# The seventh product at two levels in the paired part of a Strassen-Winograd matmul with bias and tanh

## The chip, the cores and the metric

The kernel runs on one core of one Trainium2 chip. The metric is the device time of the whole program in microseconds, over all of its work from the inputs in HBM to the stored output.

## The reference

```python
def setup_inputs():
    m, k, n = 4096, 4096, 4096
    return {
        "a": np.random.randn(m, k).astype(np.float32),
        "b": np.random.randn(k, n).astype(np.float32),
        "bias": np.random.randn(n).astype(np.float32),
    }

def reference(a, b, bias):
    return np.tanh(np.matmul(a, b) + bias)
```

## The kernel before

The product is done by Winograd's scheme: seven products, m1 to m7, of quarter-size operands take the place of eight. The output is cut into four column blocks of 1024 columns (`c` = 0 to 3, here "block 0" to "block 3") and sixteen row pairs of 256 rows. An "item" is one row pair in one column block. Its left operands are four quads (`a11`, `a12`, `a21`, `a22`, each 128 x 16 x 128 in fp16) and the sums `s1`, `s2`, `s5`, `s6`, `s7` made from them on DVE (VectorE); its right operands (`b11`, `b22`, `d1`, `d3`, `d4`, `e6`, `e7`) lie in SBUF for the whole column block. A one-level product is sixteen matmuls (`T`) of 128 x 128 by 128 x 512. When an item is met for the first time, the transposed quads are written to a DRAM scratch, with `s2` in place of `a21` and `s5` in place of `a12`; later column blocks fetch them from there.

Some products are split once more, over two items p and q = p + 1 taken together: the rows of p and q, the two halves of the inner dimension, and the two halves of the 512 columns form a 2 x 2 x 2 problem, done by seven products of eight matmuls (`TP`) with 256 columns. The left operands of this second level (`v1` to `v4`, tiles named `h`) are made by DVE for each pair by `left`, each an instruction over 128 x 1024; four places hold them, given out in turn by `place_for`. The right operands (`t1` to `t4`, "forms") are the same for all pairs of a column block. They are either kept in SBUF for the block (`kept_form`, with `t3` written over a quarter of the operand it is made from) or written to DRAM once and streamed back for each use (`put_four` makes them in a staging tile and writes them; `pull_four` fetches the next one on the GpSimd queue as soon as one of the places in `free` is let go by `multiply`).

`TWO` lists the products that are done so in the pairs that `four(n)` handles: m4 and m3 (kept forms in `g` tiles), m2 and m6 (streamed), m5 (kept). m1 and m7 are one-level there (`one_whole`), and m7 adds on to the PSUM bank `z` that holds m1, so one subtraction takes both (`take_m7`). Such pairs make up the later part of blocks 2 and 3: `FOURS`, `begins` and `ends_with` give four pairs in block 2, of which the last hands the operands back for what follows (`leave` is true; m6 and m7 are one-level in it), and six in block 3, of which the last ends the kernel (`last`).

Within `four(n)` the order of all engines' work is written out by hand: `group0` (products 1 and 2), `group1` (products 3 and 4, then two adds that it returns and that are placed later as `w`, `w2` or `u`, `u2`), and `single` for the remaining ones, named 7, 3 and 4. ScalarE copies partial sums between halves of PSUM banks, and puts zeros into a half that is to be accumulated into (`seed`). A bank half "between" holds the second product, shared by three of the four results. `take_d`, `take_c`, `take_m2`, `take_m5`, `take_m1`, `take_m6` and `take_m7` add the results into the output tiles on DVE; `end` and `result` apply tanh on ScalarE and store on the SyncE queue (SP). There are three `o` tiles for results of m2 and m5 of a pair, which need four. `left_over` carries the last steps of a pair into the next (`more`).

`turn_over(c)` is the passage from the ordinary items to these pairs; p and q there are the two items before the first pair, m the pair's first item. It has its own written-out order in which steps of the slot schedule (`at_slot`, 7 slots for an item) are called by `slot(k)`. `STAGED` gives the slots, counted from item p, at which streamed forms are made and written; those at 8 and beyond fall into `turn_over`. `M5_AT` gives the places at which m5's forms are made: negative numbers in `turn_over`, others in the first pair (`forms_at`). `M5_AWAY` is the slot at which the quarter that m5's `t3` overwrites is saved, and `BACK` the steps of the last pair of block 2 at which saved operands return.

`fetch` issues the load of a quad on SP. In `product`, an item in `early_fetch` has the `a12` of the item after next fetched right after the matmuls of m7; `after`, which follows, fetches it for the items in `twos`; p and q of a `turn_over` are in `twos`.

Of the kernel before, what the change touches and what calls it, by code (L numbers as in the profile page):

```python
# [8 lines left out]
P = 128  # L9
QP = 32  # L10
NB = 512
NCW = 2 * NB
# [107 lines left out]
def kernel(  # L120
# [471 lines left out]
    def quarter(what, r, j, i):  # L592

        return bop[TWO[what][1], 2 * r + i][:, :, HALF[j]]

    def four_right(what, name, to, made=None):
        for i in range(2):
            here = to[i] if isinstance(to, list) else to[:, ds(i * TB, TB)]
            of = made[:, ds(i * TB, TB)] if made is not None else None
# [233 lines left out]

    def place_for(what, name):
        k = left_count[0] % 4
        left_count[0] += 1
        owner[k] = what, name
        placed[what, name] = lefts[k]
        return lefts[k]

    def left(n, what, name):
        of = {"v2": "v1", "v4": "v2"}.get(name)
        if of:
            assert (what, of) in owner.values()
            of = by_four(placed[what, of])
        place = by_four(place_for(what, name))
# [12 lines left out]
    def between(n, what):  # L859
        if n not in fours:  # L860
            return bank(n, 0, "w")[:, HALF[TWO[what][3]]]
        i, where, half = {
            "m4": (n, "w", 0), "m3": (n + 1, "w", 0), "m2": (n, "w", 1), "m5": (n + 1, "w", 1),
            "m6": (n, "c", 0),
        }[what]
        return bank(i, 0, where)[:, HALF[half]]

    def multiply(n, what, to, left_, right):
        for t in range(TP):
# [5 lines left out]
            if (what, right) in rights:  # L875
                bt = rights[what, right][:, t]
            else:
# [66 lines left out]

    def m5_form(name):
        if name != "t3":
            pool, tag = (bops, "e6_1") if name == "t1" else (sums, "sum")
            rights["m5", name] = pool.tile([P, TP, NB // 2], fp16, name="form", tag=tag)
        kept_form("m5", name)

    def m5_forms(k):
        for name, at in M5_AT.items():
            if at == k:
                m5_form(name)

# [3 lines left out]
    def give_back(c, step):  # L959
        for (name, part), at in BACK.items():  # L960
            if at == step:
                if name in ("m3", "m4", "m5"):
                    move(name, c, False, part)
# [11 lines left out]
    def four(n):  # L975
# [3 lines left out]
        leave = m not in fours and not last  # L979
        homes.update({"m5": "d", "m6": "w"})  # L980
        pair = {i: items[i][1][0] for i in (p, q)}
        st = {i: state.setdefault((i, 0), {}) for i in (p, q)}
        def forms_at(k):
            if first:
                m5_forms(k)

# [4 lines left out]
        def one_whole(what, i, steps=range(T)):  # L991
            _, left_, right = next(v for v in PRODUCTS.values() if v[0] == what)
            at = "w" if what == "m6" else "z"
            whole(i, left_, right, ((bank(i, 0, at), ds(0, NB)),), what == "m6", steps)

        def end(name, i, r, j):
# [23 lines left out]

        def take_m6(i):
            tt(st[i]["s"], st[i]["s"], bank(i, 0, "w"), ADD)
            end("s", i, 1, 1)

        def take_m7(i):
            tt(st[i]["ds"], st[i]["ds"], bank(i, 0, "z"), SUB)
            end("ds", i, 0, 0)

        step(0)
        group0(n, "m4")  # L1030
        left(n, "m4", "v2")
        more()
        group0(n, "m3")
# [3 lines left out]
        w, w2 = group1(n, "m4")  # L1037
        left(n, "m3", "v3")
        w()
        left(n, "m4", "v4")  # L1040
        u, u2 = group1(n, "m3")
        step(2)
        single(n, "m4", 7)
        w2()
        left(n, "m3", "v4")
        u()
        single(n, "m3", 7)
        u2()
        forms_at(1)
        seed(p, "z", 0)  # L1050
# [12 lines left out]
        left(n, "m5", "v1")  # L1063
        forms_at(2)
        group0(n, "m2")
# [9 lines left out]
        left(n, "m2", "v3")  # L1075
        forms_at(3)
        w, w2 = group1(n, "m2")
        left(n, "m5", "v3")
        w()
        asum(p, "s1")  # L1080
# [5 lines left out]
        single(n, "m2", 7)  # L1086
        forms_at(4)
        w2()
# [20 lines left out]
        step(10)  # L1109
        one_whole("m1", p)  # L1110
        take_m5(q)
        asum(q, "s7")
        if leave:
            take_m1(p)
            if not last:
                fetch(m, "a11")
            for name in ("t1", "t2", "t4"):
                del rights["m5", name]
            step(11)
# [23 lines left out]
        left(n, "m6", "v2")  # L1143
        group0(n, "m6")
        take_m1(p)
# [7 lines left out]
        take_m1(q)  # L1153
        if last:
            for to, half in ((bank(q, 0, "z"), LAST[0]), (bank(p, 0, "c"), LAST[1])):
                tt(to[:, half], bank(q, 0, "z")[:, half], st[q]["ds"][:, half], SUB)
        else:
            fetch(m + 1, "a11")
        one_whole("m7", p)
# [7 lines left out]
        take_m6(p)  # L1167
        if not last:
            fetch(m, "a21")
            fetch(m, "a12")  # L1170
            fetch(m + 1, "a21")
            left(m, "m4", "v1")
            left(m, "m3", "v1")
            take_m6(q)
            seed(p, "w", 0)
            seed(q, "w", 0)
            seed(p, "c", 0)
            one_whole("m7", q)

            def close():  # L1180
                take_m7(q)
                fetch(m + 1, "a12")

            left_over.append(close)
            return
        take_m6(q)
        o = st[q]["ds"]
        for to, half, on in (
            (bank(q, 0, "z"), LAST[0], nc.sync), (bank(p, 0, "c"), LAST[1], nc.scalar)
        ):  # L1190
            whole(q, "s7", "e7", ((to, half),))
            nc.scalar.activation(o[:, half], to[:, half], TANH, scale=-1.0)
            on.dma_start(
                out=out[ds(2 * pair[q] * P, P), ds(c * NCW + half.start, half.size)],
                in_=o[:, half],
            )

# [24 lines left out]
    def turn_over(c):  # L1222
# [28 lines left out]
        product(q, *PRODUCTS[2])  # L1251
        m5_forms(-7)
        single(p, "m4", 3)
# [8 lines left out]
        seed(m, "d", 0)  # L1262
        m5_forms(-6)
        product(q, *PRODUCTS[5])
        fetch(m, "a21")
        slot(12)
        m5_forms(-5)
        slot(13)
        product(p, *PRODUCTS[10])
        m5_forms(-4)  # L1270
        seed(m, "w", 0)
        seed(m + 1, "w", 0)
        fetch(m, "a12")
        left(m, "m4", "v1")
        left(m, "m3", "v1")
        slot(15)
        m5_forms(-3)
        product(q, *PRODUCTS[8])
# [4 lines left out]
        slot(17)  # L1283
        m5_forms(-2)
        seed(m, "c", 0)
        product(q, *PRODUCTS[10])
        fetch(m + 1, "a12")
        free.append("sum")
        pull_four()
        m5_forms(-1)  # L1290

# [470 lines left out]
    for c in FOURS:  # L1762
        if c < NC - 1:
            at_slot(SLOTS * (begins[c] - 2) + M5_AWAY, move, "m5", c, True)

# [55 lines left out]
```

## Time and profile before

| | |
|---|---|
| Median of 3 runs | 1533.37 us (1531.91 to 1534.46) |
| Profiled execution, its own time | 1536.71 us |
| Span of the profile (first to last instruction) | 1535.0 us |
| Mean granted TensorE clock | 0.998 |
| Instructions | 23236 |
| HBM read, written | 331.88 MB, 138.94 MB |
| First pair of block 2 begins | 930.41 us |
| First pair of block 3 begins | 1256.69 us |

The profile is of one execution. Times in it are microseconds from the start of the span unless marked ns. PE is the matmul, PEld the weight load, DVE VectorE, ACT ScalarE, POOL GpSimd, SP SyncE; a "q" behind an engine's name is its instruction queue. A line number is that of the helper that issues the instruction: L475 is the one-level product of ordinary items, L940 (in `whole`) the one-level product in pairs, L879 (in `multiply`) the second-level one, L150 the DVE operation, L309 the fetch of a quad, L821 the fetch of a streamed form, L770 the write of a staged form. In a row of a timeline, "[x <-Y]" is idle time of the engine just before and what ended it. In a row of waits the three numbers are the sum, the count and the longest.

### The profile page before, as it was taken

The page shows a single profiled execution, that of the slowest core. Times are in us where ns is not written, and L with a number is a line of the kernel's source. Part 1 is how long each engine was busy: PE and PEld are TensorE (multiplying, and loading weights), DVE is VectorE, ACT ScalarE, POOL GpSimd, SP SyncE. Part 2 cuts the span into 40 slices and gives each one's busy share as a digit, 9 for nine tenths or more (in the row PEclk, how much of TensorE's full clock was granted, in tenths as well). Part 3 has the DMA queues.
Part 4 walks back from the last instruction along what each step waited for, and adds up shares of the span by engine and source line. Part 5 has one row for each costly group of instructions (what it writes and reads, how often), then busy time and mean ns, then how long its engine had stood idle before and what let it go on. Part 6 is the DMA issues. An engine that isn't in the chain of part 4 may idle for free.

```text
span 1535.0 us, 23236 instructions
## 1 busy us (share of the span) xinstructions
PE 1521.8 (99%) x8805; PEld 862.0 (56%) x8805; DVE 1120.6 (73%) x1531; ACT 361.3 (24%) x762; POOL 477.6 (31%) x868
## 2 busy tenths in 40 slices
PE   9999999999999999999999999999999999999999
PEld 4444444444445666544444556777644556777776
DVE  6789877777876666677787666777658857767777
ACT  3331111111221122111122112232222312323322
POOL 8775443334603231343551121112121211111111
PEclk9999999999999999999999999999999999999999
DMA  9999999999979998999996878899975867888895
GB/s 184 182 204 254 276 245 210 219 209 237 192 219 301 251 285 257 239 259 241 216 184 193 286 246 289 291 328 321 344 255 166 241 231 283 296 306 309 314 340 174
DMA packets 203604, 386.66 MB, mean 252 GB/s; under 512 B 25186, under 2 KB 100194, under 8 KB 203492
## 3 DMA queue, kind: packets, MB, share of 16 engines
q0 software_dynamic: 117232, 198.50, 57.1%
q1 hardware_dynamic: 85588, 186.36, 34.4%
q8 instruction: 69, 1.13, 0.3%
q10 hardware_dynamic: 672, 0.33, 0.1%
q14 instruction: 43, 0.35, 0.1%
HBM read 331.88 MB, written 138.94 MB: 307 GB/s over the span
## 4 chain that ended last, share of the span: by engine, by line
PE 96%; DMA 3%; DVE 1%; issue 0%; ACT 0%; DVEq 0%; ACTq 0%
PE ps L475 58%; PE ps L879 19%; PE ps L940 9%; PE ps L1451 5%; PE ps L672 4%; DMA a<-scratch 2%; DMA out_dram<-o 0%; DVE h L150 0%; DVE a L150 0%; DMA coarse<-in_a_dram 0%; PE warm L1511 0%; DVE form L150 0%; PE tp L1552 0%; DVE ps L150 0%; PE spread L438 0%
## 5 line engine op out<-in xcount | busy, mean ns | idle before, releaser
L475 PEld LDWEIGHTS <-a 128*128 128x128 f16 x3264 | 319.3, 98 | 378.7 <-DMA a<-scratch 0.4
L475 PE MATMUL ps<-b,a 128*128 128x512 f16 x1148 | 262.0, 379 | 0.0
L475 PE MATMUL ps<-e,a 128*128 128x512 f16 x932 | 212.1, 379 | 0.0
L475 PE MATMUL ps<-d,a 128*128 128x512 f16 x896 | 202.5, 379 | 0.0
L879 PEld LDWEIGHTS <-h 128*128 128x128 f16 x1760 | 172.2, 98 | 34.4 <-DVE h L150 10.1
L275 DVE STREAM_TRANSPOSE a<-nat 128x1024 f16<-128x1024 f16 (+2 forms) x202 | 175.3, 911 | 19.1 <-PE ps L475 17.6
L821 POOL DMA_DIRECT2D form<-form_m x133 | 70.4, 529 | 363.8 <-PE ps L879 342.5
L475 PE MATMUL ps<-d,s 128*128 128x512 f16 x656 | 148.3, 379 | 0.0
L879 PEld LDWEIGHTS <-a 128*128 128x128 f16 x1320 | 129.8, 98 | 24.7 <-issue 0.8
L475 PEld LDWEIGHTS <-s 128*128 128x128 f16 x848 | 83.0, 98 | 97.7
L247 POOL DMA_DIRECT2D nat<-in_a_dram x176 | 92.9, 533 | 134.0 <-DVE a L275 64.0
L378 POOL DMA_DIRECT2D b<-in_b_dram x192 | 103.4, 544 | 83.8 <-DVE a L275 31.0
L150 DVE TENSOR_TENSOR ps<-ps,x 128x256 f32<-128x256 f32 x128 | 54.2, 431 | 89.7 <-PE ps L879 42.3
L150 DVE TENSOR_TENSOR a<-a,a 128x2048 f16<-128x2048 f16 (+1 forms) x97 | 115.8, 1203 | 0.2
L940 PEld LDWEIGHTS <-a 128*128 128x128 f16 x688 | 66.7, 98 | 70.9 <-issue 0.3
L879 PE MATMUL ps<-form,h 128*128 128x256 f16 x768 | 98.2, 276 | 6.0 <-DVE h L150 5.8
L499 ACT ACTIVATE o<-ps 128x512 f32<-128x512 f32 x90 | 54.1, 601 | 160.9 <-issue 104.4
L940 PE MATMUL ps<-e,a 128*128 128x512 f16 (+2 forms) x360 | 77.7, 370 | 0.0
L150 DVE TENSOR_TENSOR h<-a,h 128x1024 f16<-128x1024 f16 x110 | 75.2, 685 | 0.0
L475 PE MATMUL ps<-side,a 128*128 128x512 f16 x288 | 73.9, 379 | 0.0
L940 PE MATMUL ps<-d,a 128*128 128x512 f16 x320 | 72.2, 379 | 0.0
L879 PE MATMUL ps<-form,a 128*128 128x256 f16 x536 | 70.3, 275 | 0.0
(179 smaller groups left out, 1838.5 us busy)
## 6 DMA issues: line engine op xcount, KB each, us to landing
a<-scratch SPq DMA_DIRECT2D x144, 512.0 KB, 7.0
form<-form_m POOLq DMA_DIRECT2D x133, 512.0 KB, 6.0
out_dram<-o SPq DMA_DIRECT2D x203, 256.0 KB, 5.7
nat<-in_a_dram POOLq DMA_DIRECT2D x288, 128.0 KB, 6.4
scratch<-a SPq DMA_DIRECT2D x48, 512.0 KB, 6.3
b<-in_b_dram POOLq DMA_DIRECT2D x160, 128.0 KB, 5.5
scratch<-a SPq DMA_DIRECT2D x32, 256.0 KB, 5.8
cast<-in_b_dram POOLq DMA_DIRECT2D x64, 128.0 KB, 9.1
```

The source lines that it names most:

```text
L150: nc.vector.tensor_tensor(out=out_, in0=in0, in1=in1, op=op)
L247: nc.gpsimd.dma_start(out=tl[ds(q * QP, QP), :, :], in_=src.rearrange("(mb p) k -> p mb k", p=QP),)
L275: nc.vector.transpose(dst[:, ds(b0 * tb, n * tb), :].rearrange("P (b t) (mb p) -> P mb b t p", t=tb, p=QP), src[:, :, ds(b0, n), :].rearra ...
L378: nc.gpsimd.dma_start(out=dst[ds(q * QP, QP), ds(t, nt)], in_=src)
L475: nc.tensor.matmul(st[where], at, bt, start=(what == "m2" or n < LEAD and what == "m1") and i == 0, stop=i == len(ts_) - 1, skip_group_che ...
L499: nc.scalar.activation(o, src, TANH)
L672: nc.tensor.matmul(to, at, bt, start=False, stop=t == TP - 1, skip_group_check=True)
L821: nc.gpsimd.dma_start(out=rights[what, name], in_=forms[what, name])
L879: nc.tensor.matmul(to, at, bt, start=False, stop=t == TP - 1, skip_group_check=True)
L940: nc.tensor.matmul(to[:, half], at[:, t // TB, t % TB], bop[right, t // TB][:, t % TB, half], start=anew and t == 0, stop=t == T - 1, skip ...
L1451: nc.tensor.matmul(mb[m % 4, j], aq[m, kt // T][:, kt % T, :], right(kt, j), start=fresh and kt == k0, stop=stop and kt == k1 - 1, skip_gr ...
```

## The change

m7 joins the products at two levels in the pairs of `four`. Its forms `t1` and `t2` lie in the tile `side` (the places of `b11` and `e6`, block 0), `t4` in the single `sum` tile of the pool `spare`, which was the sixth place of the streamed forms, and `t3` over a quarter of `e7`, which is saved and brought back in block 2. m7's result goes to the `d` banks, its second product to half of q's `c` bank; m1 is now taken from `z` by itself (`take_m1`, `less_m1`), and m7 by `take_m7` from `d`. Behind m1(p) the steps of m6 and m7 alternate. The places of the left operands are given out differently: `v3` takes the place of `v1`, `v4` that of `v2`. m5's forms are made earlier, four in `turn_over`; those of m7 one there and three in the first pair. The last staged forms are made at slots 4 and 7 instead of 5 and 10 (block 2) and 10 and 13 (block 3). In the pairs, the quads of the next pair are fetched earlier, `a12` of m right after the second-level matmuls that read the old one; in `turn_over` the two fetches of `a12` are taken out and m and m + 1 are put into `early_fetch`. The very end of the kernel, where the last m7 was cut into 384 and 128 columns, now ends with product 4 of m7.

```diff
-       "m2": ("s2", "b11", "z", None), "m5": ("s5", "b22", "d", None)}
+       "m2": ("s2", "b11", "z", None), "m5": ("s5", "b22", "d", None), "m7": ("s7", "e7", "d", None)}
...
-STAGED = {2: (-13, -7, -5, 0, 2, 5, 10), 3: (-8, -6, -4, 1, 10, 13)}
+STAGED = {2: (-13, -7, -5, 0, 2, 4, 7), 3: (-8, -6, -4, 1, 4, 7)}
...
-M5_AWAY = -14
+AWAY = {"m5": -14, "m7": -3}
...
-M5_AT = {"t1": -2, "t3": 1, "t2": 2, "t4": 3}
+KEPT_AT = {
+    ("m5", "t1"): -7, ("m5", "t3"): -6, ("m5", "t2"): -3, ("m5", "t4"): -1,
+    ("m7", "t1"): -4, ("m7", "t2"): 0, ("m7", "t4"): 1, ("m7", "t3"): 2,
+}
...
-    ("m4", "t3"): 5, ("m3", "t3"): 12,
+    ("m4", "t3"): 5, ("m3", "t3"): 12, ("m7", "t3"): 1,
...
-    def place_for(what, name):
-        k = left_count[0] % 4
-        left_count[0] += 1
+    def place_for(n, what, name):
+        first = {"v3": "v1", "v4": "v2"}.get(name)
+        if first and n in fours:
+            k = next(i for i in range(4) if owner.get(i) == (what, first))
+        else:
+            k = left_count[0] % 4
+            left_count[0] += 1
...
-            "m6": (n, "c", 0),
+            "m6": (n, "c", 0), "m7": (n + 1, "c", 0),
...
+    def resident(what, name):
+        if what == "m7" and name in ("t1", "t2"):
+            j = ("t1", "t2").index(name)
+            rights[what, name] = [side[:, :, ds(j * NB + i * NB // 2, NB // 2)] for i in range(2)]
+        elif name != "t3":
+            pool, tag = (bops, "e6_1") if (what, name) == ("m5", "t4") else (
+                (sums if what == "m5" else spare), "sum"
+            )
+            rights[what, name] = pool.tile([P, TP, NB // 2], fp16, name="form", tag=tag)
+        kept_form(what, name)
...
+        def take_m7(i, anew=False):
+            tt(st[i]["ds"], st[i]["ds"], bank(i, 0, "z" if leave else "d"), SUB)
+            if anew:
+                seed(i, "d", 0)
+            end("ds", i, 0, 0)
+
+        def less_m1(i):
             tt(st[i]["ds"], st[i]["ds"], bank(i, 0, "z"), SUB)
-            end("ds", i, 0, 0)
...
         single(n, "m2", 3, 4)
         step(9)
         take_m2(p)
-        asum(p, "s7")
+        asum(q, "s1")
         single(n, "m5", 3)
-        asum(q, "s1")
         if not last:
             fetch(m + 1, "a22")
         take_m2(q)
+        take_m5(p)
+        seed(p, "d", 0)
+        seed(q, "c", 0)
         asum(q, "s6")
         if not leave:
             left(n, "m6", "v1")
-        take_m5(p)
+        asum(p, "s7")
         single(n, "m5", 4)
         step(10)
         one_whole("m1", p)
         take_m5(q)
...
         left(n, "m6", "v2")
         group0(n, "m6")
+        asum(q, "s7")
+        left(n, "m7", "v1")
         take_m1(p)
         if not last:
             fetch(m, "a11")
+        left(n, "m7", "v2")
+        one_whole("m1", q)
         left(n, "m6", "v3")
-        one_whole("m1", q)
+        less_m1(p)
+        group0(n, "m7")
+        left(n, "m7", "v3")
         w, w2 = group1(n, "m6")
+        take_m1(q)
+        if not last:
+            fetch(m + 1, "a11")
+            fetch(m, "a21")
         left(n, "m6", "v4")
         w()
...
+        u, u2 = group1(n, "m7")
         if not last:
-            seed(p, "d", 0)
+            fetch(m, "a12")
+        less_m1(q)
+        left(n, "m7", "v4")
         single(n, "m6", 7)
         w2()
+        u()
+        if last:
+            single(n, "m7", 7)
+            u2()
+            here = bank(q, 0, "d")[:, HALF[0]]
+            tt(here, here, st[q]["ds"][:, HALF[0]], SUB)
...
+            single(n, "m6", 3)
+            take_m6(p)
+            single(n, "m6", 4)
+            take_m6(q)
+            single(n, "m7", 3)
+            take_m7(p)
+            single(n, "m7", 4)
+            nc.scalar.activation(o[:, HALF[0]], here, TANH, scale=-1.0)
+            store_half(o, q, 0, nc.sync)
+            return
+        single(n, "m7", 7)
+        u2()
         single(n, "m6", 3)
-        take_m7(p)
+        single(n, "m7", 3, 4)
+        fetch(m + 1, "a12")
+        seed(p, "c", 0)
+        take_m7(p, True)
+        left(m, "m4", "v1")
         single(n, "m6", 4)
...
+        fetch(m + 1, "a21")
+        take_m6(p, True)
+        take_m7(q)
+        left(m, "m3", "v1")
+
+        def close():
+            take_m6(q, True)
+
+        left_over.append(close)
...
+        early_fetch.update((m, m + 1))
...
-        fetch(m, "a12")
...
-        fetch(m + 1, "a12")
-        free.append("sum")
-        pull_four()
-        m5_forms(-1)
+        resident_at(-1)
```

More of the change, by code (lines that the diff above doesn't have):

```diff
@@ L845, in left @@
             of = by_four(placed[what, of])
-        place = by_four(place_for(what, name))
+        place = by_four(place_for(n, what, name))
         if name == "v1":
@@ L943, in whole, with resident_at @@
                 )
[L945 to L952, printed above, removed]
+    def resident(what, name):
[8 more added lines that the diff above has]
+        kept_form(what, name)
+    def resident_at(k):
+        for form, at in KEPT_AT.items():
             if at == k:
-                m5_form(name)
+                resident(*form)
     def seed(n, where, half):
@@ L994, in one_whole, with store_half @@
             whole(i, left_, right, ((bank(i, 0, at), ds(0, NB)),), what == "m6", steps)
+        def store_half(o, i, j, queue):
+            queue.dma_start(
+                out=out[ds(2 * pair[i] * P, P), ds(c * NCW + HALF[j].start, HALF[j].size)],
+                in_=o[:, HALF[j]],
+            )
         def end(name, i, r, j):
@@ L1186, in four @@
[L1186 to L1196, printed above, removed]
+        u()
[4 more added lines that the diff above has]
+            tt(here, here, st[q]["ds"][:, HALF[0]], SUB)
+            o = st[q]["ds"]
+            tt(o[:, HALF[1]], o[:, HALF[1]], bank(q, 0, "d")[:, HALF[1]], SUB)
+            nc.scalar.activation(o[:, HALF[1]], o[:, HALF[1]], TANH)
+            store_half(o, q, 1, nc.sync)
+            single(n, "m6", 3)
[8 more added lines that the diff above has]
+            return
@@ L1266, in turn_over @@
         slot(12)
-        m5_forms(-5)
+        resident_at(-5)
         slot(13)
         product(p, *PRODUCTS[10])
-        m5_forms(-4)
+        resident_at(-4)
         seed(m, "w", 0)
         seed(m + 1, "w", 0)
-        fetch(m, "a12")
         left(m, "m4", "v1")
@@ L1763 @@
         if c < NC - 1:
-            at_slot(SLOTS * (begins[c] - 2) + M5_AWAY, move, "m5", c, True)
+            for what, at in AWAY.items():
+                at_slot(SLOTS * (begins[c] - 2) + at, move, what, c, True)
     handed = {s for c in FOURS for s in range(SLOTS * (begins[c] - 2) + 8, SLOTS * ends_with[c])}
```

63 lines of the change are left out of this document (21 added, 42 removed).

## The prediction

> **What bounds the kernel.** I read the page first, then the chain of work in order of time, then a table by stage over the two-level pairs, then the timelines of each engine inside one of them.
>
> ```profile
> span 1535.0 us, 23236 instructions
> PE 1521.8 (99%) x8805; PEld 862.0 (56%) x8805; DVE 1120.6 (73%) x1531; ACT 361.3 (24%) x762; POOL 477.6 (31%) x868
> PE 96%; DMA 3%; DVE 1%; issue 0%; ACT 0%; DVEq 0%; ACTq 0%
> ```
>
> TensorE is on the chain 96% of the time, so work taken from it counts in full as long as nothing else becomes late. The next table cuts two-level pairs into stages: the first column is the stretch, then its length, then busy time of PE, PEld, DVE, ACT and POOL, the granted clock, and DMA.
>
> ```profile
> 1398.96:1443.34 44.38, 44.38 (x347) 33.66 (x345) 32.90 (x52) 13.10 (x33) 7.41 (x14) 1.00 0.86 308
> 1256.70:1310.20 53.50, 48.28 (x347) 35.02 (x346) 41.19 (x66) 14.85 (x38) 9.51 (x18) 0.94 0.79 277
> ...
> 1398.80:1412.77 13.97, 13.97 (x129) 12.53 (x128) 9.01 (x16) 4.26 (x12) 0.94 (x2) 1.00 0.73 283
> 1412.77:1423.25 10.48, 10.48 (x98) 9.39 (x96) 8.75 (x15) 2.97 (x8) 2.77 (x6) 1.00 0.84 287
> 1423.25:1443.18 19.93, 19.93 (x123) 11.75 (x120) 15.14 (x23) 5.87 (x14) 3.70 (x7) 1.00 0.96 338
> 944.39:958.75 14.36, 11.32 (x99) 9.05 (x96) 12.44 (x21) 2.54 (x8) 2.75 (x6) 1.00 0.73 252
> 1273.35:1290.09 16.74, 13.55 (x99) 10.79 (x96) 13.03 (x21) 2.94 (x8) 2.76 (x6) 0.80 0.59 188
> ```
>
> An ordinary pair takes 44.38 us and PE is busy for all of it. Its last three rows of stages are m4 and m3 (13.97), m2 and m5 (10.48), and m1, m6, m7 (19.93). The first pair of column block 3 takes 53.50, 9.1 more; the m2/m5 stage alone takes 16.74 there. In block 2 the same stage takes 14.36, 3.9 more than 10.48.
>
> **The change: matmuls.** Pieces of the chain (start, length, what):
>
> ```profile
> 1398.96 24.45 PE ps L879 x224
> ...
> 1433.82 3.45 PE ps L940 x16
> ```
>
> A 256-column matmul takes 24.45/224 = 0.109 us, a product of sixteen 512-column ones 3.45. m7 of a pair is two such products, 6.90 us; at two levels it is 7 x 8 matmuls of 256 columns, 6.11 us. Block 2 has three such pairs (the fourth hands back and keeps the one-level m7), block 3 has six: **9 x 0.79 = 7.1 us less**.
>
> The Trainium skill, "TensorE: Matmul & The Clock Gate", section "Back-to-back issue gap", speaks against this: it gives sustained spacings of 81 ns for 128 columns and 131 ns for 512, so about 98 ns for 256 as an estimate, by which 56 x 98 ns would be more than 32 x 131 ns. The two rows above measure both shapes here, 109 and 216 ns, and the measurement decides.
>
> **DVE in the new tail.** Starts, durations and waits on DVE in an ordinary pair (m1 of p starts on PE at 1423.25; I count t from there):
>
> ```profile
> 1421.95 0.68 DVE L150 TENSOR_TENSOR ds<-ds,ps 128x512 f32<-128x512 f32 x1
> 1422.54 2.36 DVE L150 TENSOR_TENSOR a<-a,a 128x2048 f16<-128x2048 f16 x2
> 1424.81 0.69 DVE L150 TENSOR_TENSOR ds<-ds,ps 128x512 f32<-128x512 f32 x1
> ...
> 1428.98 0.69 DVE L150 TENSOR_TENSOR o<-s,ps 128x512 f32<-128x512 f32 x1 [0.43 <-DMA out_dram<-o]
> 1429.59 0.68 DVE L150 TENSOR_TENSOR ds<-ds,ps 128x512 f32<-128x512 f32 x1
> ...
> 1431.32 0.69 DVE L150 TENSOR_TENSOR h<-a,h 128x1024 f16<-128x1024 f16 x1
> 1431.92 0.68 DVE L150 TENSOR_TENSOR s<-s,ps 128x512 f32<-128x512 f32 x1
> ...
> 1438.18 0.43 DVE L150 TENSOR_TENSOR ps<-ps,x 128x256 f32<-128x256 f32 x1 [2.63 <-PE ps L879]
> 1438.52 0.68 DVE L150 TENSOR_TENSOR ds<-ds,ps 128x512 f32<-128x512 f32 x1
> ```
>
> From start to start a staged left or a 512-column take costs 0.60, a whole sum (s1, s6, s7) 1.13, a small add 0.34. The change adds per pair four lefts (2.4), two adds (0.7) and two takes of m1 apart from m7 (1.2): 4.3 us on 32.9 of 44.4, giving 37.2 of 43.6. DVE is not the bound on average; order decides.
>
> The new PE order in t: m1(p) 0 to 3.45, m6's first two 5.20, m1(q) 8.65, m7's first two 10.40 (the second, on v1, from 9.52), m6's next two 12.14, m7's 13.89, the two sevens 15.63, m6's three 16.51, m7's three and four 18.25, m6's four 19.13. The next pair starts at 19.13 in place of 19.93.
>
> DVE up to m7's v1: take_m2(p) at -1.30 as now, s1(q) -0.70, take_m2(q) 0.43, take_m5(p) 1.03, s6(q) 2.23, m6 v1 3.36 to 4.05 (PE needs it at 4.33), s7(p) to 5.09. take_m5(q) can start at 5.09, but its output buffer is the one that take_m2(p) is storing from: in the quoted pair the store had landed at W = 1428.98 - 1423.25 = 5.73. Then 1.2 for take_m5(q), 0.6 for m6 v2, 1.13 for s7(q), 0.7 for m7 v1: ready at W + 3.6, with PE wanting it at about 9.4. Today W = 5.3 + the wait that the view shows, and a wait up to 0.5 is free in the new order; more is PE idle. The waits in the ordinary pairs of block 2, of block 3, and in the pair that hands back:
>
> ```profile
> DVE o L150 <- DMA out_dram<-o: 1.7, 2, 1.4
> ...
> DVE o L150 <- DMA out_dram<-o: 2.0, 3, 0.8
> ...
> 1099.74 0.69 DVE L150 TENSOR_TENSOR o<-s,ps 128x512 f32<-128x512 f32 x1 [2.88 <-DMA out_dram<-o]
> ```
>
> (us, times, longest.) Block 2: 1.4 and 0.3, so 0.9 lost; block 3: 0.8, 0.8 and 0.4, so 0.6: **1.5 us given back**. If no store were late it is 0; if all were as late as the last row, 2.4 in each pair.
>
> After m7 v1 every left is early: m7 v2 is done at 10.5 (needed 13.0), v3 at 12.3 (14.8), v4 at 15.0 (16.5); the shared third x is free after w2 at 15.4, so u ends at 16.3, needed at 16.5. take_m7(p) follows m7's three by about 0.2, as the add at 1438.18 follows its seven: 17.6 to 18.3, the seed of d on ACT to 18.7, before the next pair's 19.13. take_m6(p) ends at 19.5 and its seed at 19.9, needed at 20.0; take_m6(q) at 21.3, its seed 21.7, needed at 21.75. These margins are 0.1; I charge 0.1 a pair, **0.8**, with 0 and 0.4 a pair as ends. The 1.9 us by which DVE enters the next pair later fall into its idle time there.
>
> **Queues.** On SP the fetches of a21 and a12 of m now wait for m6 v4 and m7 v4 (t 13.5 and 15.0) with only the fetches and stores of the tail behind them; before, they left at 17.7 or later, so they land earlier. POOL streams the forms of m2 and m6 through five places instead of six. The tightest are then the sixth and seventh of m2, asked for 8.5 us before their use; at that point of the pair they land in:
>
> ```profile
> DMA to landing us min/median/max: 3.5/4.2/4.9
> ...
> DMA to landing us min/median/max: 3.4/5.6/8.9
> ```
>
> That costs nothing; the longest of the second row, which is over the ordinary pairs of block 3, would cost under 1 us each.
>
> **The first pairs.** Lines of DVE, SP and PE around the change-over into block 3, then of block 2:
>
> ```profile
> 1256.76 1.29 DVE L150 TENSOR_TENSOR stage<-e,stage 128x1024 f16<-128x1024 f16 x2 [9.53 <-DMA form_m<-stage]
> ...
> 1276.83 0.69 DVE L150 TENSOR_TENSOR h<-a 128x1024 f16<-128x1024 f16 x1 [4.09 <-DMA a<-scratch]
> ...
> SPq L309 <- DMA a<-scratch: 9.1, 1, 9.1
> ...
> 1261.40 10.58 DMA a<-scratch
> 1272.00 4.81 DMA a<-scratch
> ...
> PE ps L879 <- DVE h L150: 3.2, 1, 3.2
> PE ps L879 <- ACT ps L957: 1.9, 1, 1.9
> ...
> SPq L309 <- DMA a<-scratch: 14.1, 2, 8.0
> ...
> 933.08 9.00 DMA a<-scratch
> 942.09 4.19 DMA a<-scratch
> ...
> PE ps L879 <- DVE h L150: 2.7, 2, 1.6
> ```
>
> In block 3 DVE stands 9.53 us before a staged form whose predecessor is still being written out. Everything behind it is late: the take of m7, the seeds (1.9 us of PE), the stores ahead of the last fetches on SP. The new STAGED slots (4 and 7 in place of 10 and 13) take this wait away. The second stall comes from a12 of m+1. It is fetched twice into one tile, by `after` and again by `turn_over`, so the second waits for the first (9.1 us on SP), lands 4.81 later, and only then can DVE form m5's v1. The change drops the call in `turn_over`, but sets `early_fetch`, so `product` and `after` now both fetch: **still two**. With SP free earlier I get: a12(m) behind m7(p), which ends two products (6.9) before the pair begins at 1256.7, so at 1250; its double 8 later at 1258, two stores, a21 and a12 of m+1 at 1259.6, landed 9.0 to 10.6 later, the double another 4.2 to 4.8: 1272.8 to 1275.0. PE wants m5's v1 at 1256.7 + 13.97 + 0.87 = 1271.5 and gets it 0.75 after the landing: 2.0 to 4.2 idle, where it is 3.2 plus 1.9 now. The m7 t3 form (1.3 us) delays m2's v4 by 0.8, and small margins take 0.5. So about 4.2 of the 9.1 stay: **4.9 less**. The forms of m5 move ahead of the pair, where DVE waits for PE anyway, and four of m7 come in; five of these eight now lie before the pair, and the two lefts they delay wait for fetches anyway. Block 2 has no long staged wait and the same double fetch (8.0 on SP, then 4.19), so its loss stays: **0.2 less**, between 2 more and 2 less.
>
> The clock was 0.80 over the 16.74 us: 3.3 us lost beside the 3.2 idle. A wait of 1.6 us in block 2 left it at 1.00. The Trainium skill, same page, Part 1 ("The HAM clock gate"), has the clock halve after an idle window of 3.4 us that runs freely; the trace agrees (3.2 tripped it, 1.6 did not), and by it my 2.0 to 4.2 may go either way.
>
> **The end.** After the last matmul there now stand m7's take of p, two tanh and two stores, where today there is one tanh of 128 columns:
>
> ```profile
> 1531.29 0.49 ACT L1192 ACTIVATE ds<-ps 128x384 f32<-128x384 f32 x1 [1.25 <-PE ps L940]
> 1532.18 0.28 ACT L1192 ACTIVATE ds<-ps 128x128 f32<-128x128 f32 x1 [0.40 <-PE ps L940]
> ```
>
> p's take ends as the last matmul does, its tanh takes 0.6, the other 0.35, so the last store leaves 0.6 later than now after the last matmul: **0.6 given back** (0 to 1).
>
> **Sum.** -7.1 + 1.5 + 0.8 + 0.6 - 4.9 - 0.2 = -9.3. Against the profiled execution (1536.7, with 1.7 around its span) that is 1527.4; against the median of the runs, 1533.4, it is 1524.1. The median lies 3.3 below the profiled run, as much as the half clock cost, so ordinary runs may not have it; then 1527.3. I take 1525.0; its own range is 1521 to 1529.
>
> **Rivals.** (a) The first pairs come clean: with SP early enough both doubles are hidden. Then 9.1 and 4.2 go, but for 1: -16.5, 1517. For it: the stalls are set by a single landing. Against: both fetches stay. (b) The half clock trips in both first pairs: block 3 gains 1.7, block 2 loses 3.1: 1530.6. For it: block 2 idles a little longer, block 3 is near 3.2. (c) Slower: the store of take_m2(p) sets m7 v1 in every pair. If DVE's wait is 2.9 each time, as in the pair that hands back, 9 x 2.4 = 21.6 is lost instead of 1.5: 1544. It outweighs everything from a mean wait of 1.7. For it: the DMA share is 0.96 in this stage. Against: five waits of seven, none over 1.4. (d) The change gains nothing in the first pairs and head margins cost 0.4: 1531 to 1534. (e) 256-column matmuls cost too much per instruction, as the quoted section would have it: break-even is 6.90/56 = 0.123 us, and with its spacings the time is about 1543; the chain's 0.109 leaves it no chance.
>
> **Chances.** Forecast 0.54, (a) 0.10, (b) 0.14, (c) 0.10, (d) 0.12, (e) 0. The range 1517.5 to 1532.5 takes in the forecast, (b), half of (a) and most of (d). Beyond 0.2% (3.1 us, about what a measurement of this kernel can tell from no change): faster 0.79, within 0.10 (part of (d) and (b)), slower 0.11.
>
> **What would show it.** Ordinary pairs of 43.6 us, with PE waiting on DVE h by fractions; no DVE wait on a staged form in the change-over; the second a12 fetch still waiting on SP for the first, and PE idle 2 to 4 us at m5's v1 in both first pairs. Pairs over 44.4 would prove me wrong by (c); first pairs under 46, by (a).

## The result and the profile after

The median fell from 1533.02 us (four runs, 1531.91 to 1534.46) to **1521.9 us** (four runs, 1520.41 to 1523.23): ratio 0.9927, 95% interval 0.9909 to 0.9944, so 11 us or 0.73% faster. The profiled execution took 1522.57 us, its span 1520.6. Of all executions reported below, one, of the change with the old slots, took 2678.31 us at a granted clock of 0.556, and its kernel's ratio leaves it out.

The head of the page after: the span, the busy times, and the chain that ended last.

```profile
span 1520.6 us, 23784 instructions
PE 1509.8 (99%) x9005; PEld 878.9 (58%) x9005; DVE 1166.8 (77%) x1619; ACT 377.1 (25%) x809; POOL 479.1 (32%) x868
PE 91%; DMA 4%; DVE 3%; POOL 1%; issue 0%; ACT 0%; DVEq 0%; SPq 0%; ACTq 0%; POOLq 0%
```

DVE has 46 us more to do and TensorE 12 us less, in more and shorter matmuls. TensorE is still the bound, but its share of the chain fell from 96% to 91%: what is left of waiting sits mostly in transfers (4%) and DVE (3%).

The table by stage after, with the columns of the prediction's. Its rows are, in order: an ordinary pair of block 3, the first pair of block 3, the m2/m5 stage of block 2's first pair, the m4/m3 stage and the m2/m5 stage of block 3's first pair, and a pair of block 3 with a wait.

```profile
1296.18:1339.77 43.59, 43.59 (x371) 35.97 (x368) 36.94 (x61) 14.73 (x39) 7.43 (x14) 1.00 0.90 324
1250.29:1296.18 45.89, 44.38 (x369) 35.70 (x368) 40.11 (x66) 12.86 (x34) 6.89 (x13) 1.00 0.84 278
...
942.85:954.29 11.44, 10.85 (x98) 9.22 (x96) 11.23 (x19) 2.61 (x8) 2.77 (x6) 1.00 0.79 269
1250.29:1264.46 14.17, 14.13 (x129) 12.53 (x128) 11.22 (x20) 4.26 (x12) 0.94 (x2) 1.00 0.68 227
1264.46:1276.85 12.39, 10.94 (x98) 9.23 (x96) 11.23 (x19) 2.61 (x8) 2.78 (x6) 1.00 0.85 270
...
1339.77:1383.87 44.10, 43.77 (x371) 35.94 (x369) 36.84 (x61) 14.74 (x39) 7.43 (x14) 1.00 0.87 307
```

An ordinary pair went from 44.38 to 43.59, the 0.79 of two products in smaller pieces. The first pair of block 3 went from 53.50 to 45.89, its m2/m5 stage from 16.74 to 12.39, and the clock in it is 1.00 where it was 0.80. The same stage of block 2 went from 14.36 to 11.44. In the pair of 44.10, m7's v1 (the first left operand of the second-level m7) comes late. Four of TensorE's five waits on DVE in block 3 after, from its timeline:

```profile
1266.37 1.05 PE L889 MATMUL ps<-form,h 128*128 128x256 f16 x8 [0.87 <-DVE h L153]
1273.24 1.05 PE L889 MATMUL ps<-form,h 128*128 128x256 f16 x8 [0.59 <-DVE h L153]
1374.25 1.05 PE L889 MATMUL ps<-side,h 128*128 128x256 f16 x8 [0.33 <-DVE h L153]
1461.98 1.05 PE L889 MATMUL ps<-side,h 128*128 128x256 f16 x8 [0.36 <-DVE h L153]
```

The first two rows are m5's v1 and m2's v4 in the first pair; the other two (`side` holds m7's first forms) are m7's v1, and a fifth like them, of 0.36, is in the last pair. Ahead of the late v1 of 1374.25, DVE stands at the take of m5, whose output tile is still being stored:

```profile
1370.44 0.69 DVE L153 TENSOR_TENSOR o<-s,ps 128x512 f32<-128x512 f32 x1 [0.91 <-DMA out_dram<-o]
```

In the five pairs behind the first these waits of DVE are 0.34, 0.91, 0.42, 0.94 and 0.94. The two short ones cost TensorE nothing, the three long ones 0.33 to 0.36. In DVE's list of waits (us, times, longest) the staging tile has shrunk to

```profile
DVE stage L153 <- DMA form_m<-stage: 0.8, 1, 0.8
```

where one wait in the passage was 9.53. SP's queue around the change-over after (start, length, what), and then the chain there:

```profile
1250.64 0.86 SPq L493 DMA_DIRECT2D out_dram<-o  x2
1251.60 9.76 SPq L312 DMA_DIRECT2D a<-scratch  x3
```

```profile
1252.19 8.83 DMA a<-scratch
1261.04 4.56 DMA a<-scratch
```

The three fetches take 9.76 us to issue because the last of them waits for the transfer before it: a12 of m + 1 is still fetched twice into one tile, 8.83 us and then 4.56.

**The budget of the profiled span, 14.4 us less.** From matmul to matmul the first pair of block 3 went from 53.35 to 45.89 and that of block 2 from 48.40 to 44.98: beside the 0.79 of the matmuls that is 6.7 and 2.6 less. The nine pairs give 7.1 less. Three waits at m7's v1 cost 0.5 each, the pair that hands back 0.5 (TensorE waits 0.41 for a left there, not followed further), the end 1.9. And block 2's pairs begin at 928.67 in place of 930.41, a lead of 1.7 that is there by 90 us, where the change touches nothing, so it is a difference between executions. -6.7 - 2.6 - 7.1 + 1.5 + 0.5 + 1.9 - 1.7 = -14.2. Without the start it is -12.5, beside -11.1 in the medians; the profiled run of before was 3.7 above its median.

### The profile page after: what moved, and what is told of

It reads as the page before. It is cut to its first block, busy times and chain, and to the rows that moved or that the text cites. A ratio compares the mean times of both kernels' runs of the same rounds, so it can differ in the third digit from the quotient of the medians.

```text
span 1520.6 us, 23784 instructions
## 1 busy us (share of the span) xinstructions
PE 1509.8 (99%) x9005; PEld 878.9 (58%) x9005; DVE 1166.8 (77%) x1619; ACT 377.1 (25%) x809; POOL 479.1 (32%) x868
## 4 chain that ended last, share of the span: by engine, by line
PE 91%; DMA 4%; DVE 3%; POOL 1%; issue 0%; ACT 0%; DVEq 0%; SPq 0%; ACTq 0%; POOLq 0%
PE ps L478 58%; PE ps L889 21%; PE ps L1488 4%; PE ps L950 4%; PE ps L678 4%; DMA a<-scratch 2%; DMA out_dram<-o 1%; DVE h L153 1%; DVE a L153 1%; DVE ps L153 0%; DMA land<-in_a_dram 0%; DVE ds L153 0%; DMA side<-in_b_dram 0%; POOL land L1529 0%; POOL side L1577 0%
## 5 line engine op out<-in xcount | busy, mean ns | idle before, releaser
L478 PEld LDWEIGHTS <-a 128*128 128x128 f16 x3264 | 319.2, 98 | 379.0 <-DMA a<-scratch 0.5
L889 PEld LDWEIGHTS <-h 128*128 128x128 f16 x2048 | 199.2, 98 | 31.8 <-DVE h L153 6.3
L889 PEld LDWEIGHTS <-a 128*128 128x128 f16 x1536 | 150.3, 98 | 24.0
L153 DVE TENSOR_TENSOR ps<-ps,x 128x256 f32<-128x256 f32 x146 | 60.8, 429 | 60.2 <-ACT x L895 32.8
L153 DVE TENSOR_TENSOR h<-a,h 128x1024 f16<-128x1024 f16 x128 | 86.7, 684 | 0.0
L889 PE MATMUL ps<-form,a 128*128 128x256 f16 x608 | 77.5, 273 | 0.0
L153 DVE TENSOR_TENSOR ds<-ds,ps 128x512 f32<-128x512 f32 (+1 forms) x94 | 63.6, 678 | 17.3 <-PE ps L889 7.0
L153 DVE TENSOR_TENSOR h<-a 128x1024 f16<-128x1024 f16 x80 | 54.7, 688 | 16.4 <-DMA a<-scratch 15.7
```

Of the source, the lines that this page charges most:

```text
L153: nc.vector.tensor_tensor(out=out_, in0=in0, in1=in1, op=op)
L478: nc.tensor.matmul(st[where], at, bt, start=(what == "m2" or n < LEAD and what == "m1") and i == 0, stop=i == len(ts_) - 1, skip_group_che ...
L889: nc.tensor.matmul(to, at, bt, start=False, stop=t == TP - 1, skip_group_check=True)
```

## Experiments

The ordinary pairs need no more explanation. The first pairs do: 9.3 us came from two of them, where 5.1 was forecast. Theory A: the new slots of the staged forms did it, by taking DVE's 9.53 us at a staged form (the "staged wait" below) out of the passage. Theory B: the earlier making of m5's forms did it. Theory C: the landing times scatter, and most of it is luck. What remains in these pairs should be the doubled fetch. Excess of the first pair over an ordinary pair of the same kernel (44.38 or 43.59), in block 2 and in block 3, was 4.0 and 9.0 before, 1.4 and 2.3 after. Each excess is read from one profiled run, and the one of before lies 3.7 us above its median and holds the half clock. So the medians say what an edit is worth, and the excess says where.

**The change with the old slots.**

```diff
-STAGED = {2: (-13, -7, -5, 0, 2, 4, 7), 3: (-8, -6, -4, 1, 4, 7)}
+STAGED = {2: (-13, -7, -5, 0, 2, 5, 10), 3: (-8, -6, -4, 1, 10, 13)}
```

> The changed kernel with the staged forms at their former slots (the last ones at 5 and 10 in block 2, at 10 and 13 in block 3). Theory A, the staged slots give what the first pairs gained beyond the matmuls (6.8 us in block 3, 2.8 in block 2): DVE again stands about 9 us before a staged form in the passage into block 3, the first pair there is back at 50 to 53 us (45.9 in the changed kernel), that of block 2 at 46 to 48 (45.0), and the time is 5 to 9 us above the changed kernel, about 1528. Theory B, the earlier forms of m5 give it: under 1.5 us of difference. Theory C, it is all in the second-level m7 and in scatter: no difference.

1530.55 us beside 1533.77 of before, ratio 0.9975 (0.9966 to 0.9984). Without the new slots the change keeps 3 to 4 of its 11 us, so they carry 7 to 8. DVE around the change-over, from its timeline:

```profile
1253.40 1.29 DVE L153 TENSOR_TENSOR stage<-e,stage 128x1024 f16<-128x1024 f16 x2 [6.72 <-DMA form_m<-stage]
1273.27 0.69 DVE L153 TENSOR_TENSOR h<-a 128x1024 f16<-128x1024 f16 x1 [3.42 <-DMA a<-scratch]
```

Both old stalls are back, at 6.72 and 3.42 us where the kernel before had 9.53 and 4.09. Excess 3.3 and 6.2.

**The kernel before with the new slots alone** (the same edit the other way).

> The kernel before with the staged forms at the new slots and nothing else. Theory A: the DVE wait of 9.5 us goes, the first pair of block 3 falls from 53.5 to about 47, that of block 2 by about 2, and the time falls by 5 to 9 us, to about 1526. Theory B (the earlier forms of m5): the first pairs stay within 1.5 us of what they were, 1532 to 1533.

1527.93, ratio 0.9957 (0.9944 to 0.9970). The staged wait is 0.7, and the left that had waited 4.09 us for the doubled fetch waits 1.13:

```profile
1269.78 0.69 DVE L150 TENSOR_TENSOR h<-a 128x1024 f16<-128x1024 f16 x1 [1.13 <-DMA a<-scratch]
```

Excess 2.5 and 2.0: one line of slot numbers gives 5.8 us, most of it in block 3.

**The kernel before with m5's forms made early.**

```diff
-M5_AT = {"t1": -2, "t3": 1, "t2": 2, "t4": 3}
+M5_AT = {"t1": -7, "t3": -6, "t2": -3, "t4": -1}
...
-            pool, tag = (bops, "e6_1") if name == "t1" else (sums, "sum")
+            pool, tag = (bops, "e6_1") if name == "t4" else (sums, "sum")
```

> The kernel before with the forms of m5 made in the passage as in the changed kernel (t1, t3, t2, t4 in this order, t4 in the place that t1 had), nothing else. Theory A: no more than 1 us either way, since the passage into block 3 still waits for the staged form; the added DVE work may even make the seeds later. Theory B: the first pairs lose most of their excess, 1525 to 1528.

1532.48, ratio 0.9993 (0.9984 to 1.0003): no measurable gain, although the excess is 1.1 and 5.5 in the profiled run (1528.89, its fastest of twelve up to 1536.86). The staged wait is still there (longest 7.8), and now it holds the very first products. TensorE in the timeline, and then two stretches in the table of windows:

```profile
1252.37 1.04 PE L879 MATMUL ps<-d,a 128*128 128x256 f16 x8
1255.64 1.03 PE L879 MATMUL ps<-g,h 128*128 128x256 f16 x8 [2.23 <-ACT ps L957]
1256.74 1.80 PE L879 MATMUL ps<-d,a 128*128 128x256 f16 x8
1258.34 1.91 PE L879 MATMUL ps<-g,h 128*128 128x256 f16 x8
```

```profile
1252.00:1258.00 6.00, 3.70 (x26) 2.61 (x25) 5.24 (x9) 2.31 (x6) 1.70 (x4) 0.90 0.49 145
1258.00:1262.00 4.00, 4.00 (x28) 3.10 (x27) 3.27 (x6) 0.94 (x3) 0.42 (x1) 0.72 1.00 366
```

TensorE waits 2.23 us for a seed, and then eight matmuls that take 1.04 take 1.80 and 1.91. So in this run the early forms shorten block 2's first pair, where the excess fell from 4.0 to 1.1, and leave most of block 3's. The median shows no gain, and since this run was 3.6 us faster than it, the excess of an ordinary run may be larger; no run here shows where.

**Both edits in the kernel before**, m7 still at one level.

> The kernel before with both the new slots of the staged forms and the earlier forms of m5; m7 stays one-level. If the first pairs' gain is these two together, the first pair of block 2 takes about 45.5 us and that of block 3 about 46.3, the ordinary pairs stay at 44.38, and the time is near 1525; the changed kernel is then below it by what m7 brings net: 7.1 less for the matmuls, 1.6 back for stores that land late, 1.9 back at the end, about 3.5 us. If the second-level m7 with its order shortens the first pairs by itself, this kernel stays near the 1528 of the new slots alone.

1523.92, ratio 0.9942 (0.9928 to 0.9955): 8.8 of the 11 us without the change's title. Excess 0.0 and 2.6. Block 2 shows what each edit does. TensorE's waits on a left in the m2/m5 stage of its first pair, first in the kernel before (two rows: m5's v1 and m2's v4), then with the new slots alone, then with the early forms alone:

```profile
947.06 1.05 PE L879 MATMUL ps<-form,h 128*128 128x256 f16 x8 [1.63 <-DVE h L150]
955.14 1.05 PE L879 MATMUL ps<-form,h 128*128 128x256 f16 x8 [1.02 <-DVE h L150]
```

```profile
953.76 1.05 PE L879 MATMUL ps<-form,h 128*128 128x256 f16 x8 [1.02 <-DVE h L150]
```

```profile
944.52 1.05 PE L879 MATMUL ps<-form,h 128*128 128x256 f16 x8 [0.93 <-DVE h L150]
```

The early forms take away the wait at m2's v4, which stood behind a form made in the stage. The new slots take away the wait at m5's v1: DVE starts this left 14.4 us into the pair instead of 15.9, and 14.4 instead of 16.4 in the change with the new slots and the old. With both edits TensorE waits for neither. By which path the slots bring the fetch forward in block 2 is not shown.

C, scatter alone, falls: the gains stand in the medians, outside their intervals. But landing times do scatter. In block 3, DVE starts m5's v1 between 13.7 and 16.3 us into the first pair in five profiles with the new slots and the doubled fetch, and between 19.2 and 20.1 in three with the old slots. So the sizes of single waits in one profile are partly luck. What m7 itself gives, with the new order around it, is the difference to the whole change, 2.0 us in the medians, where about 3.5 was expected (3.6 between the two profiled runs from the first pair on), and 1.9 between the early forms alone and the change with the old slots.

**The change with one fetch of each a12.**

```diff
-        early_fetch.update((m, m + 1))
```

> The changed kernel with a12 of the first pair fetched once instead of twice in each passage (m and m + 1 are not put into the list that makes the product fetch it too). By the prediction the second fetch, which waits for the first and lands 4.6 us after it, sets the start of m5's v1: without it DVE has no wait there, PE no idle time before m5's second product in block 3 (0.9 us shown, 1.0 with the rest), and the first pair of block 3 takes about 44.5 us instead of 45.9, that of block 2 about 44.5 instead of 45.0: 1.0 to 2.5 us less, about 1520. If instead DVE's backlog behind the new forms sets it (the 0.6 us waits before m2's v4 in both blocks), the first pairs stay within 0.5.

1520.28, ratio 0.9914 (0.9901 to 0.9926). Excess 0.5 and 0.2; the first pair of block 3 and its m4/m3 and m2/m5 stages:

```profile
1249.89:1264.02 14.13, 14.09 (x129) 12.49 (x128) 12.59 (x23) 4.26 (x12) 0.90 (x2) 1.00 0.45 181
1264.02:1274.50 10.48, 10.48 (x98) 9.39 (x97) 10.09 (x17) 2.93 (x8) 2.81 (x6) 1.00 0.82 278
1249.89:1293.68 43.79, 43.75 (x370) 36.01 (x369) 40.18 (x66) 12.93 (x34) 6.88 (x13) 1.00 0.77 279
```

The m2/m5 stage is at its 10.48 again, so in this profile the doubled fetch was almost all that was left in block 3. Two kernels below keep the doubled fetch and show 1.2 and 0.8 there instead of 2.3, so its price varies from run to run; in the medians it is 1.6 us.

**The kernel before with one fetch of each a12.**

```diff
-        fetch(m, "a12")
         left(m, "m4", "v1")
...
-        fetch(m + 1, "a12")
         free.append("sum")
```

> The kernel before with a12 of m and of m + 1 fetched once in the passage. If the doubled fetch is a cause by itself, the a12 of m + 1 lands 4.8 us earlier in block 3 and 4.2 in block 2, the stall of 3.2 us and the half clock behind it (3.3) go and 1.9 stay: 6.5 less in block 3, 2.5 less in block 2, 1524 to 1525. If the staged form's wait of 9.5 us is what matters, because it makes SP late anyway, a wait of 1 to 3 us stays before m5's first form: 3 to 5 less in all, 1528 to 1530. If both had only one cause, nothing changes: 1533.

1525.8 beside 1533.13, ratio 0.9954 (0.9941 to 0.9967). The doubled fetch was a cause by itself, though the staged wait stayed almost whole. DVE, then what TensorE loses to it:

```profile
1251.35 1.29 DVE L150 TENSOR_TENSOR stage<-e,stage 128x1024 f16<-128x1024 f16 x2 [8.61 <-DMA form_m<-stage]
...
1254.23 1.03 PE L879 MATMUL ps<-g,h 128*128 128x256 f16 x8 [0.99 <-ACT ps L957]
1275.24 1.05 PE L879 MATMUL ps<-form,h 128*128 128x256 f16 x8 [0.37 <-DVE h L150]
```

Excess 0.8 and 2.3. So DVE's wait of 8.6 us costs TensorE little when the fetches behind it are not doubled, and the doubling costs less when DVE does not wait (at m5's v1 TensorE lost nothing with the new slots alone, 2.07 with both edits): each of the two edits alone, slots or fetch, takes 7.0 or 6.7 us off block 3's excess of 9.0, because most of the stall needed both. In the medians, block 2 included, the slots give 5.8 us and the single fetch 7.3.

**The change with a later take of m5.** `take_m5(q)` stands behind m7's v1, as its output tile is the one that is late.

```diff
         single(n, "m5", 4)
         step(10)
         one_whole("m1", p)
-        take_m5(q)
         if leave:
+            take_m5(q)
...
         left(n, "m7", "v1")
+        take_m5(q)
         take_m1(p)
```

> The changed kernel with the take of m5 for q moved behind m7's v1 on DVE (in pairs where m7 is two-level). The prediction holds that the store of m2's result for p, whose buffer this take needs, sets the start of m7's v1: three ordinary or last pairs of block 3 show PE idle 0.33 to 0.36 there and take 44.1 us instead of 43.58. With the move v1 is ready at about 7.5 us after m1 of p begins, 2 before its use, these idle times go and all ordinary pairs take 43.58: 1.0 to 1.6 us less than the changed kernel, if nothing else becomes late. If DVE's amount of work and not the store sets it, the waits come back at another left and the time stays.

1520.19, ratio 0.9917 (0.9903 to 0.9930). No wait at m7's v1 is left; of TensorE's waits on a left only those in the first pairs remain:

```profile
PE ps L889 <- DVE h L153: 1.1, 2, 0.6
```

That is 3.5 in seven waits in the change as it is; the last pair and the end together became 0.7 shorter. The median is 1.7 below the change's. The profile's first pairs are shorter too, with an excess of 1.2 in both blocks, and the edit acts only behind the stages in which they lose their time, so part of the 1.7 may be scatter.

**The change with p's last take in two halves**, the first of them ahead of m6's seventh product.

```diff
+        if last:
+            take_half(p, 0)
         single(n, "m6", 7)
...
-            take_m7(p)
+            take_half(p, 1)
```

> The changed kernel with the last take of m7 for p done in two halves of the columns, the first as soon as that half is complete. The changed kernel needs 4.7 us from the end of its last matmul to the end of the span, against 2.8 before. If that is the 512-column take, tanh and store of p queued ahead of the last half, 0.5 to 1.0 us go. If it is the landing of the stores, no more than 0.2.

1523.12, ratio 0.9933 (0.9921 to 0.9946): nothing is gained. The last steps of the change, and then of this kernel, from the timelines:

```profile
1514.85 1.04 PE L889 MATMUL ps<-form,a 128*128 128x256 f16 x8
1514.93 1.23 ACT L1018 ACTIVATE s<-s 128x512 f32<-128x512 f32 x2 [0.18 <-DVE s L153]
1515.42 0.68 DVE L153 TENSOR_TENSOR ds<-ds,ps 128x512 f32<-128x512 f32 x1
1516.13 0.63 ACT L1018 ACTIVATE ds<-ds 128x512 f32<-128x512 f32 x1
1516.67 0.37 ACT L1216 ACTIVATE ds<-ps 128x256 f32<-128x256 f32 x1
1517.21 0.41 SPq L1012 DMA_DIRECT2D out_dram<-ds  x1
```

```profile
1515.75 1.04 PE L889 MATMUL ps<-form,a 128*128 128x256 f16 x8
1516.17 1.23 ACT L1018 ACTIVATE s<-s 128x512 f32<-128x512 f32 x2 [0.18 <-DVE s L153]
1516.65 0.41 DVE L153 TENSOR_TENSOR ds<-ds,ps 128x256 f32<-128x256 f32 x1
1517.30 0.40 ACT L1057 ACTIVATE ds<-ds 128x256 f32<-128x256 f32 x1
1517.61 0.36 ACT L1224 ACTIVATE ds<-ps 128x256 f32<-128x256 f32 x1
```

In both, ScalarE runs nearly without a gap from the two tanh of m6's results on, and those start where DVE's takes of m6 let them. The very last tanh starts 0.78 and 0.82 after the modelled end of the last matmul: the half take shortened DVE's last step and moved the work, not the end.

**One fetch, late take and halves together.**

> The changed kernel with one a12 fetch in each passage, the take of m5 for q behind m7's v1, and the last take in halves. If the three are independent: 1.6 (measured) + 1.0 to 1.6 + 0.5 to 1.0 us below the changed kernel, 1517.5 to 1519. If the late stores and the end share one cause with the fetches (the load on the DMA engines), it is no better than one fetch alone, 1520.

1518.15, ratio 0.9904 (0.9891 to 0.9918): 3.8 us below the median of the change. One fetch and the late take alone gave 1.6 and 1.7, so they add up, and the halves add nothing that can be told.

**The same, with the very last store on ScalarE's queue.**

```diff
-            store_half(o, q, 0, nc.sync)
+            store_half(o, q, 0, nc.scalar)
```

> The version with one fetch, the late take and the halves at the end, and its very last store is issued on ScalarE's queue in place of SP's. At the end of the changed kernel 3.4 us pass from the issue of the last store to the end of the span (1517.21 to 1520.6), where the kernel before has 2.5 (1532.49 to 1535.0) with its last store on ScalarE's queue. If the queue makes the difference (the last of five stores in a row on SP), the last store is issued right behind its tanh and the span ends 2.5 later: 0.8 to 1.2 us less, 1517.1. If the size of the store makes it (128 KB against 64 KB), nothing is gained: 1518.2. Either way the three edits together stay below the changed kernel by 3 to 5.

1518.31, ratio 0.9905 (0.9889 to 0.9920): nothing is gained. Its last store is issued at

```profile
1513.55 0.36 ACTq L1012 DMA_DIRECT2D out_dram<-ds  x1
```

and the span ends at 1516.9, 3.35 later, as with SP's queue (3.4) and not 2.5. So the queue alone does not make the end longer.

**And without the halves.**

> The same with the last take of m7 for p whole again, as the change has it: one fetch, the late take, the last store on ScalarE's queue. It shows what the halves are worth where DVE reaches the end earlier than in the changed kernel: if ScalarE's order sets the end (five tanh behind each other), the halves are worth nothing and this kernel equals the other of this call; if DVE's last take does, it is 0.4 us slower.

1518.59, ratio 0.9907 (0.9893 to 0.9921): the median does not tell the halves' worth from nothing here either. In its profile the last store is issued at 1512.78 and the span ends at 1517.4, 4.6 us later on the same queue and with the same size, so this last stretch scatters by more than a us. All twelve runs of these last three kernels lie between 1517.10 and 1519.65, all four of the change between 1520.41 and 1523.23. The version to keep is the change with one fetch and the late take; it was run here only with its last store on ScalarE's queue.

## Why the prediction was right, point by point

The prediction of 1525.0 was 3.1 too high, inside both its ranges, and no term had the wrong sign, though block 2's first pair went from the smallest to the third largest. Its sum of -9.3 would have been -12.5 with the measured terms. That the total came so near is partly luck: the two first pairs gave 4.2 us more than forecast and the heads cost 0.8 less, while the end and the pair that hands back, which the forecast put at nothing, cost 1.8 more.

- **Matmuls**, -7.1: as measured, 44.38 to 43.59 a pair. Rival (e), dearer small matmuls, would have made the pair longer.
- **Late stores**, +1.5: three of nine pairs lost 0.5. The forecast had them in some pairs and not in others, and so it was, with about 0.5 of DVE's wait free as worked out; the late take removed them.
- **Heads**, +0.8: mis-sized. The pair of 43.59 has TensorE busy for all of it, so margins of 0.1 held.
- **First pair of block 3**, -4.9: the staged wait went and the doubled fetch stayed, as worked out. The size was off: I had the fetches of m + 1 leave 2.9 us into the pair and the double land at 16.1 to 18.3. They left at 1.9 (1252.19) and it landed at 15.3 (1265.60). That leaves m5's v1 0.87 late, where I had 2.0 to 4.2; m2's v4 behind the new t3 form is 0.59 late, where I had 0.8. The term measured -6.7. (The pieces of the forecast's rest, with the middle of 2.0 to 4.2, add up to 4.4 and not to 4.2.)
- **First pair of block 2**, -0.2: the step that failed. I held that with no long staged wait there, the double fetch would set it as before. With the double fetch in place, the new slots took its excess from 4.0 to 2.5, the early forms to 1.1, both to 0.0. So the loss had two parts: the double fetch, which the new slots did bring forward here too, by 1.4 to 2.0 us at m5's v1, and m5's forms made inside the m2/m5 stage, whose move I had priced at nothing and which held m2's v4 back by 1.02. The term measured -2.6.
- **End**, +0.6: mis-sized, 1.9 by the modelled ends of the last matmuls (2.86 from there to the end of the span, now 4.71). I had p's take end with the last matmul; it runs in DVE's queue behind m6's two takes, and the tanh of four results behind each other make the last one start 0.78 after that end instead of 0.04. From the last store's issue to the end of the span it is then 3.4 in place of 2.5. The new last store is 128 KB instead of 64 KB, the queue alone is not the reason, and a smaller last store was not tried, so the cause of this part stays open.
- **The rivals**: both first pairs are under 46 us, which was to be the mark of (a), both doubles hidden. In block 2 the double was hidden, in block 3 all but 0.87 of it, so the result lies between the forecast and (a). The clock of (b) stayed at 1.00. Of (c), a late store in every pair, there were three pairs in nine, waiting 0.33 to 0.36. The first pairs gained 9.3, so (d) is out.

## What to carry to other kernels

When a change has a title, look for its one-line companions: here two lists of slot numbers gave four fifths of the gain, and one of them gave half of the gain alone. Where one wait stands ahead of another, as DVE's behind a staging tile and SP's behind a doubled fetch, removing either may remove most of the loss, so their prices don't add. A step that moves off the critical stage is not free of value because the engine has time on average: price it in the stage that it leaves.

## What the runs showed of the hardware

The clock fell after less idling than I had thought. In the kernel before with early forms, TensorE waited 2.23 us up to 1255.64, ran eight matmuls at full speed, and then had a granted clock of 0.72 from 1258 to 1262. A wait of 2.07 us in the kernel with both edits left the granted clock of that pair at 1.00, from TensorE's timeline and from the table of windows:

```profile
1271.16 1.05 PE L879 MATMUL ps<-form,h 128*128 128x256 f16 x8 [2.07 <-DVE h L150]
```

```profile
1254.08:1301.09 47.01, 44.73 (x345) 33.50 (x344) 35.31 (x57) 12.94 (x33) 7.40 (x14) 1.00 0.85 294
```

The Trainium skill, "TensorE: Matmul & The Clock Gate", Part 1 ("The HAM clock gate"), asks for an idle window of about 3.4 us that runs freely; 2.23 us of idling is less than one such window, so here the trace does not agree with that length. The 3.2 us of the kernel before, which the prediction took for agreement, is shorter than one window too. Whether a wait of 2 to 3 us trips it can't be told from its length alone in these runs.
